# SwiGLU gate and up products as block products in seven multiplications, with the hidden layer kept in DRAM

## The chip, the cores and the metric

The kernel runs on one core of a Trainium2 chip. The metric is device time in microseconds of that core; three runs of the kernel before took 2433.13, 2434.04 and 2437.89 us, median 2434.04. A core has five engines that run side by side and meet at semaphores: TensorE (PE) multiplies, and loads its stationary operand by instructions of its own (PEld); VectorE (DVE), ScalarE (ACT) and GpSimd (POOL) do elementwise work; SyncE (SP) issues most DMAs. Each engine takes its instructions in the order in which the program has them. TensorE reads from SBUF and writes to PSUM, which has 8 banks of 512 fp32 columns.

## The reference

Two layers over 1088 tokens (1024 of a prompt, 64 of eight sample sequences), 1024 features. Layer 0 mixes by convolution and an RWKV-7 recurrence, layer 1 by causal window averages. Each is followed by a SwiGLU feed-forward network of 2816 hidden features, which is what changes here:

```
def swiglu(x, wg, wu, wd):
    return (jax.nn.silu(x @ wg) * (x @ wu)) @ wd
...
x = layer_norm(ALPHA * x + mix, p['ln_mix_g'][i], p['ln_mix_b'][i])
x = layer_norm(ALPHA * x + swiglu(x, p['ffn_gate'][i], p['ffn_up'][i], p['ffn_down'][i]),
               p['ln_ffn_g'][i], p['ln_ffn_b'][i])
```

## The kernel before

Every wide product is made of three: each operand is split into a rounded part (hi, a ScalarE copy into the type fp32r) and the rest (lo, a subtraction), and hi x hi, hi x lo and lo x hi are summed in PSUM. `split` does it for activations (subtraction on VectorE), `load_w` for weights (subtraction on GpSimd).

The program has these parts, in this order on TensorE. `phase1` and `phase2` hold the input projection, the convolution and the recurrence; phase 2 is ordered by hand on TensorE and leaves nine token tiles `y` (128 tokens by 1024 features, the last one 64 tokens) in SBUF, normalized. `feat_hl` transposes them (`ft`), applies the LayerNorm's gain and bias on ScalarE and splits them into feature-major operands for three token blocks of 384, 384 and 320 columns.

`ffn` then goes through the 22 hidden tiles in 11 groups of two. For a hidden tile and a token block, `gate_up` makes 24 products for gate (`f_g`) and 24 for up (`f_u`), silu on ScalarE, the multiplication and the split of `h` on VectorE; `down` multiplies the group's `h` by the down weights (`dn`, 512 columns wide) for all nine token tiles and adds the result to `y` on VectorE, group after group. So every weight is loaded once per layer, and `h` stays in SBUF. The first and last groups go block by block of tokens. In layer 0 the last group is followed, block by block, by `finish` (LayerNorm of the tile), `pool_tile` (layer 1's mixer: products `pp` and `pl`, with a halo of 16 tokens from the tile before) and `feat_hl` for layer 1.

The order on each engine comes from the framework's scheduler, which ranks instructions by program order and by its own estimate of when they can run; names below carry tile and group numbers. The lines of the helpers: L58 is every product, L55 every ScalarE copy, L74 the weight subtraction, L79 the activation subtraction, L1001 the product with silu, L1029 the addition to `y`, L114 gain and bias of `y` on GpSimd, L92, L98, L108 and L109 the LayerNorm.

Of the kernel before, what the change touches and what calls it, by code (L numbers as in the profile page):

```python
# [21 lines left out]
TOK = SEQ + NS * LS  # L22
FF = 2816
# [21 lines left out]
class Prog:  # L45
# [11 lines left out]
    def mm(self, out, lhsT, rhs, start=True, stop=True):  # L57
        self.nc.tensor.matmul(out, lhsT, rhs, start=start, stop=stop)  # L58
# [22 lines left out]
    def rsqrt_var(self, out, var, eps, n, name):  # L81
        """out[:, :n] = (var + eps) ** -0.5"""
# [22 lines left out]
    def layernorm(self, y, n, g, b, name):  # L105
        """y[:n] <- LayerNorm over its 1024 columns"""
# [4 lines left out]
    def affine(self, y, n, g, b, engs):  # L111
        """y[:n] <- y * gain + bias (token-major, both broadcast over the tokens)"""
# [3 lines left out]
    def load_gb(self, which):  # L116
        g = self.gb.tile([128, D], F32, tag="g", name=f"g_{which}")
        b = self.gb.tile([128, D], F32, tag="b", name=f"b_{which}")
# [4 lines left out]
    def feat_hl(self, blk, which, xb):  # L123
        """feature-major (hi, lo) of LayerNorm number `which` of the normalized y tiles of a block"""
        nc = self.nc
        n0, n = NBLK[blk]
        xh, xl = xb[blk]
        for k in range(KT):
            ps = self.psum("o" if which else "ch", f"ft{which}_{blk}_{k}")
            for i in range(3 * blk, 3 * blk + 3):  # L130
                t0, m = TT_TILES[i]
                nc.tensor.transpose(ps[:, t0 - n0:t0 - n0 + m], self.y[i][:m, k * 128:(k + 1) * 128], self.ident[:m, :m])
            t = self.ftmp.tile([128, 384], F32, tag="ft", name=f"fx{which}_{blk}_{k}")
            nc.scalar.activation(out=t[:, :n], in_=ps[:, :n], func=AF.Identity, scale=self.v("lng", which * 8 + k),
                                 bias=self.v("lnb", which * 8 + k))
            self.split(xh[:, k, :], xl[:, k, :], t[:, :n])
# [16 lines left out]
    # ------------------------------------------------------------------ consts  # L153
    def consts(self, es):
# [5 lines left out]
        self.wraw = pool("wraw", 2)  # L160
        self.wring, self.wi = [pool("wring", 2)], 0
        self.first = {4: self.load_w(I["w_in"][4].rearrange("p k f -> p (k f)"), "in4", nc.vector)}
        self.ident = cp.tile([128, 128], F32, name="ident")
# [10 lines left out]
    # ------------------------------------------------------------------ phase 1  # L174
    def phase1(self):
# [3 lines left out]
        # 0.5 * (w0, a0, ka, conv ln gain, conv ln bias, conv taps); 1 - 0.5 * ka  # L179
# [48 lines left out]
        def conv_tile(ct):  # L228
            # the tanh of the gate is written where the product with the values then goes
# [32 lines left out]
            with tc.high_priority(offset=-self.LATE):  # L262
# [6 lines left out]
                # the sample tokens: all taps of 2 sequences at once  # L269
# [100 lines left out]
    def conv_b(self, i):  # L370
        """affine part and silu, feature-major, (hi, lo)"""
# [20 lines left out]
    def wout(self, i, get, w, alpha, after=None):  # L392
        """y[i] <- alpha * y[i] + half of the output projection (alpha None: 1)"""
# [25 lines left out]
    def convs(self, wA):  # L419
        """the steps of the conv branch, in one slot per token tile and two more, each stage a slot behind the one before"""  # L420
# [560 lines left out]
    def ffn(self, l, xb, affine, finish, after):  # L981
# [49 lines left out]
        for gi, fs in enumerate(groups):  # L1031
# [11 lines left out]
            if last:  # L1043
                ldown()
                for b in range(3):
                    for f in fs:
                        gate_up(f, b, w[f, "gate"], w[f, "up"])
                    for i in range(3 * b, 3 * b + 3):
                        down(fs, i, wd, last)
                        if i == 8:  # L1050
                            self.fold(l)
# [270 lines left out]
```

## Time and profile before

| | us |
|---|---|
| median of three runs | 2434.04 |
| span of the profiled execution, first to last instruction | 2432.7 |
| TensorE busy | 2312.4 (95%) |
| VectorE busy | 1206.4 (50%) |
| GpSimd busy | 863.9 (36%) |
| ScalarE busy | 622.3 (26%) |

The profiled execution is one run of the same program; its span leaves out what lies before the first and behind the last instruction. A share of 95% for TensorE is a mean over parts that differ: in the feed-forward parts it is busy without a gap, in the recurrence it often waits. A busy time counts overlapping products once, so the price of a product is read from how often one starts, not from its own duration. The page's chain gives the path that ended last: dn 22%, f_u 21%, f_g 21%, all on TensorE.

### The profile page before, as it was taken

To read this page: it belongs to the slowest core of one execution; us is meant where nothing else is said; L and a number is where in the kernel's file an instruction comes from. 1 tells how busy PE (TensorE), PEld (TensorE's weight loads), DVE (VectorE), ACT (ScalarE), POOL (GpSimd) and SP (SyncE) were. 2 spreads that over 40 slices of the span, in tenths; PEclk is the share of its full clock that TensorE was granted. 3 is DMA by queue.
4 is the path that set the end of the run, shared out by engine and by line. 5 is a ranking of instruction groups with operands and counts; after the bars stand their busy time and mean duration, and the time that the engine had idled before them with its cause. 6 is when DMAs were issued, how large, how long until landed. Compare 5 with 4: busy or idle time off the path is not lost.

```text
span 2432.7 us, 34066 instructions
## 1 busy us (share of the span) xinstructions
PE 2312.4 (95%) x13970; PEld 2087.6 (86%) x13970; DVE 1206.4 (50%) x1907; ACT 622.3 (26%) x1273; POOL 863.9 (36%) x729
## 2 busy tenths in 40 slices
PE   8898898869988999999999999999999999999997
PEld 7887786757756999999999999898999999999996
DVE  6987798725688432223333234884232333222337
ACT  3243345445525211111111111242111111111110
POOL 3589866543317412222211222455221211222212
PEclk9998898869989999999999999999999999999999
DMA  5132427735411211111111110112111111111101
GB/s 164 47 119 70 127 77 233 229 80 154 128 48 52 76 35 53 53 35 53 40 48 35 53 52 21 53 35 70 53 48 40 53 35 35 53 53 35 52 18 74
DMA packets 132199, 169.56 MB, mean 70 GB/s; under 512 B 52229, under 2 KB 99517, under 8 KB 132036
## 3 DMA queue, kind: packets, MB, share of 16 engines
q1 hardware_dynamic: 128990, 160.15, 21.5%
q10 hardware_dynamic: 3054, 7.24, 0.8%
q8 instruction: 109, 1.79, 0.3%
q14 instruction: 46, 0.38, 0.0%
HBM read 133.43 MB, written 34.15 MB: 69 GB/s over the span
## 4 chain that ended last, share of the span: by engine, by line
PE 75%; DVE 12%; POOL 5%; issue 3%; ACT 2%; DMA 2%; SPq 0%; POOLq 0%; DVEq 0%; ACTq 0%
PE dn L58 22%; PE f_u L58 21%; PE f_g L58 21%; DVE acc L268 4%; PE wo L58 2%; PE in L58 1%; PE pp L58 1%; PE po_t L58 1%; POOL X L620 1%; PE pl L58 1%; POOL xt L618 1%; DVE f38l L79 1%; DVE xt L618 1%; DVE f40l L79 1%; PE pc_t L58 1%
## 5 line engine op out<-in xcount | busy, mean ns | idle before, releaser
L58 PE MATMUL dn<-hl_d,h 128*128 128x512 f32 (+1 forms) x2288 | 565.4, 395 | 1.6 <-DVE y L1029 1.6
L58 PEld LDWEIGHTS dn<-hl_d,h 128*128 128x128 f32 (+1 forms) x2288 | 420.3, 186 | 94.0 <-DVE y L1029 2.5
L1029 DVE TENSOR_TENSOR y<-y,dn 128x512 f32<-128x512 f32 x360 | 231.0, 682 | 323.6 <-PE dn L58 322.2
L1001 DVE TENSOR_TENSOR sg<-sg,f_u 128x384 f32<-128x384 f32 x132 | 70.1, 531 | 564.6 <-PE f_u L58 558.3
L74 POOL TENSOR_TENSOR hl_d<-raw_d,hl_d 128x1024 fp32r<-128x1024 f32 x44 | 111.6, 2558 | 529.5 <-ACT hl_d L55 529.5
L58 PE MATMUL in<-xh,hl_in 128*128 128x384 f32 (+1 forms) x1056 | 282.4, 348 | 17.4 <-ACT xh L55 9.0
L74 POOL TENSOR_TENSOR hl_gate<-raw_gate,hl_gate 128x1024 fp32r<-128x1024 f32 x44 | 106.1, 2412 | 513.4 <-ACT hl_gate L55 513.4
L1000 ACT ACTIVATE sg<-f_g 128x384 f32<-128x384 f32 x132 | 62.4, 473 | 669.1 <-PE f_g L58 669.0
L58 PEld LDWEIGHTS in<-xh,hl_in 128*128 128x128 f32 x1056 | 199.1, 201 | 30.0 <-ACT xh L55 9.0
L79 DVE TENSOR_TENSOR h<-sg,h 128x384 fp32r<-128x384 f32 (+2 forms) x176 | 166.4, 964 | 81.0 <-ACT h L55 81.0
L268 DVE SCALAR_TENSOR_TENSOR acc<-u,hv,acc 128x1024 f32<-128x1024 f32 x120 | 193.2, 1620 | 0.8
L58 PE MATMUL in<-xl,hl_in 128*128 128x384 f32 (+1 forms) x528 | 182.9, 346 | 0.5 <-DVE xl L79 0.5
L55 ACT ACTIVATE h<-sg 128x384 fp32r<-128x384 f32 (+2 forms) x176 | 70.4, 423 | 314.6 <-DVE sg L1001 314.6
L74 POOL TENSOR_TENSOR hl_up<-raw_up,hl_up 128x1024 fp32r<-128x1024 f32 x44 | 105.9, 2407 | 36.5 <-ACT hl_up L55 36.4
L58 PEld LDWEIGHTS in<-xl,hl_in 128*128 128x128 f32 x528 | 105.5, 200 | 3.6 <-issue 1.8
L58 PE MATMUL f_g<-f37h,hl_gate 128*128 128x384 f32 x352 | 95.9, 342 | 2.3 <-ACT sg L1000 1.2
L58 PE MATMUL f_u<-f37h,hl_up 128*128 128x384 f32 x352 | 97.7, 337 | 0.0
L58 PE MATMUL f_u<-f43h,hl_up 128*128 128x384 f32 x352 | 97.1, 337 | 0.0
L58 PE MATMUL f_u<-f39h,hl_up 128*128 128x384 f32 x352 | 95.8, 342 | 0.0
L58 PE MATMUL f_g<-f43h,hl_gate 128*128 128x384 f32 x352 | 94.9, 339 | 0.0
L58 PE MATMUL f_g<-f39h,hl_gate 128*128 128x384 f32 x352 | 94.6, 338 | 0.0
L58 PE MATMUL f_g<-f45h,hl_gate 128*128 128x384 f32 x352 | 94.1, 338 | 0.0
(428 smaller groups left out, 4803.9 us busy)
## 6 DMA issues: line engine op xcount, KB each, us to landing
raw_gate<-ffn_gate SPq DMA_DIRECT2D x44, 512.0 KB
raw_up<-ffn_up SPq DMA_DIRECT2D x44, 512.0 KB
raw_d<-ffn_down SPq DMA_DIRECT2D x44, 512.0 KB
raw_in<-w_in SPq DMA_DIRECT2D x22, 512.0 KB
ATm_t<-atd SPq DMA_DIRECT2D x16, 512.0 KB
y<-x SPq DMA_DIRECT2D x8, 512.0 KB
AR_t<-ard SPq DMA_DIRECT2D x8, 512.0 KB
BKh_t<-bkd SPq DMA_DIRECT2D x8, 512.0 KB
```

The lines of the kernel that those rows point to most:

```text
L55: self.nc.scalar.activation(out=out, in_=in_, func=AF.Copy)
L58: self.nc.tensor.matmul(out, lhsT, rhs, start=start, stop=stop)
L74: (eng or nc.gpsimd).tensor_tensor(out=hl[:, 1, :], in0=raw, in1=hl[:, 0, :].bitcast(F32), op=ALU.subtract)
L79: (eng or self.nc.vector).tensor_tensor(out=out_lo, in0=src, in1=out_hi.bitcast(F32), op=ALU.subtract)
L268: nc.vector.scalar_tensor_tensor(out=out, in0=src, scalar=cw(j), in1=out, op0=ALU.mult, op1=ALU.add)
L618: eng.tensor_tensor(out=xs, in0=X[:P, :m, s:s + 1].to_broadcast([P, m, w]), in1=At[:P, s:s + 1, s + 1:].to_broadcast([P, m, w]), op=ALU.mult)
L620: eng.tensor_tensor(out=nx, in0=nx, in1=xs, op=ALU.add)
L1000: nc.scalar.activation(out=t, in_=pg[0][:, :n], func=AF.Silu)
L1001: nc.vector.tensor_tensor(out=t, in0=t, in1=pg[1][:, :n], op=ALU.mult)
L1029: nc.vector.tensor_tensor(out=ys, in0=ys, in1=ps[half][:n], op=ALU.add)
```

## The change

The two weight matrices and the activations of the gate and up products are cut into 2 x 2 blocks: a pair of hidden tiles (2 x 128 features) by two halves of the 1024 input features, and two halves of the input features by two halves of the tokens (544 each). The product of the blocks is made with Strassen's scheme in Winograd's form: seven block products instead of eight, with four sums of weight blocks (`s1` to `s4`, per pair and matrix) and four of activation blocks (`t1` to `t4`, per layer). Every block product is again hi x hi, hi x lo, lo x hi, on two PSUM banks of 272 columns.

`h` is written to DRAM tile by tile (`hd`). The down products come after all of gate and up: three groups of three token tiles, each with its sums in six PSUM banks over all 22 hidden tiles, and for every group the down weights are loaded and split again. Between phases, `y` and its transposed form go through DRAM as well (`yd`, `xtd`), where before they stayed in SBUF.

```
+    def product(self, ps, op, x, start, stop):
+        for k in range(4):
+            for i, (a, b) in enumerate(((0, 0), (0, 1), (1, 0))):
+                for s in range(2):
+                    self.mm(ps[s][:, :TQ], op[:, a, k * 128:(k + 1) * 128], x[:, b, k, s * TQ:(s + 1) * TQ],
+                            start and k == 0 and i == 0, stop and k == 3 and i == 2, skip_group_check=not start)
+    def operand(self, src, name):
+        hl = self.hlp.tile([128, 2, 512], F32R, tag="op", name=f"op_{name}")
+        self.split(hl[:, 0, :], hl[:, 1, :], src)
+        return hl
+    def late_x(self, l, pool):
...
+        for k in range(4):
+            xf = [self.rawp.tile([128, 2, TH], F32, tag="rw", name=f"xl{l}_{k}{j}") for j in range(2)]
+            for j in range(2):
+                nc.sync.dma_start(out=xf[j], in_=self.xtd[l][j][:, k::4, :])
...
+            t1 = diff("t1", xf[1][:, 0], xf[0][:, 0])
+            t2 = diff("t2", xf[1][:, 1], t1)
+            diff("t3", xf[1][:, 1], xf[1][:, 0])
+            put("b22", xf[1][:, 1])
+            diff("t4", xf[0][:, 1], t2)
+    def emit(self, l, p, mat, blk, s, src):
...
+            nc.scalar.activation(out=self.sg[key], in_=src, func=AF.Silu)
+        else:
+            t = self.sg.pop(key)
+            nc.vector.tensor_tensor(out=t, in0=t, in1=src, op=ALU.mult)
+            c0 = (blk % 2) * TH + s * TQ
+            nc.scalar.dma_start(out=self.hd[l][2 * p + blk // 2][:, c0:c0 + TQ], in_=t)
+    def first_two(self, l, p, mat, a11, a12, between=None):
...
+        pa = [self.psum("mm", f"pa{nm}{s}") for s in range(2)]
+        self.product(pa, self.operand(a11, f"a11_{nm}"), self.X["b11"], True, True)
...
+            self.copy_act(c1[s], pa[s][:, :TQ])
...
+        self.product(pa, self.operand(a12, f"a12_{nm}"), self.X["b21"], False, True)
+    def gate_up(self, l, p, mat, c1=None):
...
+            s1 = comb("s1", a21, a22, ALU.add)
+            s2 = comb("s2", s1, a11, ALU.subtract)
...
+            self.product(ps["b"], self.operand(s2, f"s2_{nm}"), X["t2"], True, True)
...
+                nc.vector.tensor_tensor(out=u2[s], in0=c1[s], in1=ps["b"][s][:, :TQ], op=ALU.add)
+            self.product(ps["c"], self.operand(s1, f"s1_{nm}"), X["t1"], True, True)
...
+                self.copy_act(c5[s], ps["c"][s][:, :TQ])
...
+        self.product(ps["b"], self.operand(s3, f"s3_{nm}"), X["t3"], False, True)
...
+        self.product(ps["c"], self.operand(s4, f"s4_{nm}"), X["b22"], False, True)
+        for s in range(2):
+            out(3, s, c5[s], u3[s])
+            out(1, s, u2[s], ps["c"][s][:, :TQ])
+        self.product(pd, self.operand(a22, f"a22_{nm}"), X["t4"], True, True)
+        for s in range(2):
+            out(2, s, u3[s], pd[s][:, :TQ])
+    EARLY = 2
+    def stage1_early(self, l):
+        self.early_x(l)
+        for p in range(self.EARLY):
+            for mat in ("gate", "up"):
...
+                self.c1[p, mat] = self.first_two(l, p, mat, raw[:, :512], raw[:, 512:])
+    def stage2(self, l, gb, finish):
...
+        for g in ((0, 1, 2), (3, 4, 5), (6, 7, 8)):
...
+                ps[i] = [self.psum(("mm", "o", "ch")[j], f"dn{l}_{i}_{x}") for x in range(2)]
+                self.y[i] = self.yp.tile([128, D], F32, tag="y", name=f"yr{l}_{i}")
+                nc.sync.dma_start(out=self.y[i][:TT_TILES[i][1]], in_=self.yd[l][i][:TT_TILES[i][1]])
+                self.affine(self.y[i], TT_TILES[i][1], *gb, (nc.gpsimd, nc.gpsimd))
+            for f in range(NF):
...
+                nc.sync.dma_start(out=raw, in_=I["ffn_down"][l, f])
+                wd = self.wdp.tile([128, 2, 1024], F32R, tag="wd", name=f"hl_d{l}_{f}_{t0}")
+                self.split(wd[:, 0, :], wd[:, 1, :], raw)
...
+                nc.sync.dma_start(out=hr[:, :n], in_=self.hd[l][f][:, t0:t0 + n])
...
     def build(self):
...
+            e1.close()
+            self.rawp = pool("raws", 4)
+            self.hlp = pool("ops", 7)
...
+            for l in range(2):
+                self.stage1_early(l)
+                self.stage1(l)
...
+                    if l == 0:
+                        self.pool_weights(self.gb)
...
+                    self.stage2(l, g0, finish)
```

`early_x` loads and splits the two blocks that need only the first half of the tokens (`b11`, `b21`); `first_two` of the first two pairs uses these alone, and comes ahead of `late_x`. `finish` holds the LayerNorm of a tile and, in layer 0, `pool_tile`, the normalization and `xt` (transposes, gain and bias, the write to `xtd`).

The first place at which the order changes is TensorE where the recurrence ends and the first feed-forward part begins. Before, with `wo` the output projection of the last token tile, `ft` the transposes and `f_0_0_g` the gate products of the first hidden tile and token block:

```order
L58 MATMUL wo_36_7322<-hl_woB_5467,bhl_7323 64x512
L132 MATMUL ft_0_2_7433<-ident,y_3956 128x128
L132 MATMUL ft_0_2_7433<-ident,y_3957 128x128
L132 MATMUL ft_0_2_7433<-ident,y_3958 128x128
...
L58 MATMUL f_0_0_g<-f37h_7411,hl_gate_0_7614 128x384
L58 MATMUL f_0_0_g<-f38l_7412,hl_gate_0_7614 128x384
L58 MATMUL f_0_0_g<-f37h_7411,hl_gate_0_7614 128x384 x2
```

Now, with `xt_8` the transposes of the last token tile and `pa_0g` the first block product of gate:

```order
L60 MATMUL wo_36_7551<-hl_woB_5533,bhl_7552 64x512
L135 MATMUL xt_7_0_7594<-ident,y_4029 128x128
...
L135 MATMUL xt_8_0_7617<-ident,y_4030 128x64
L135 MATMUL xt_8_1_7628<-ident,y_4030 128x64
...
L60 MATMUL pa_0g_7697<-b_0_7669,op_a_0_0g 128x272
L60 MATMUL pa_0g_7698<-b_0_7669,op_a_0_0g 128x272
```

Before, gate products of the first block start while later tiles are still being transposed; now the first block product stands behind the transposes of the last tile.

The second place is ScalarE where layer 0's gate and up end and the down products begin. Before, around a group of down products, `hl_d` are the down weights and `h` the hidden tile:

```order
L55 ACTIVATE hl_gate_3_8152<-raw_gate_3_8150 128x1024
L55 ACTIVATE hl_up_3_8157<-raw_up_3_8155 128x1024
L1000 ACTIVATE sg_2_0_8211<-f_2_0_g 128x384
L55 ACTIVATE hl_d_2_8502<-raw_d_2_8500 128x1024
L55 ACTIVATE hl_d_3_8507<-raw_d_3_8505 128x1024
L55 ACTIVATE h_2_0_8210<-sg_2_0_8211 128x384
```

Now, at the change of stage, with `hd` the writes of `h` and `hl_pw` the mixer's weights of layer 1:

```order
L1069 DMA hd_20_116<-sg_10_11_12949 128x272
L57 ACTIVATE hl_d_0_0_13310<-raw_d_0_0_13308 128x1024
L57 ACTIVATE hl_d_1_0_13338<-raw_d_1_0_13336 128x1024
L1069 DMA hd_21_117<-sg_10_20_12981 128x272
L1069 DMA hd_21_117<-sg_10_21_12984 128x272
L57 ACTIVATE hl_pw_13281<-raw_pw_13274 128x1024
L57 ACTIVATE hl_pw_13285<-raw_pw_13276 128x1024
L57 ACTIVATE h_0_0_13315<-hr_0_0_13313 128x384
```

The copy of the first hidden tile, `h_0_0`, now stands behind the last writes of `h` and behind the mixer's weights.

The third place is TensorE behind the last down products of layer 0. Before, with `pp` and `pl` the mixer's products for the last tile and `f_1_0` the products of layer 1's first hidden tile:

```order
L58 MATMUL f_1_0_u<-f43h_12979,hl_up_1_14272 128x384
L58 MATMUL pl_0_13985<-hl_pw_12973,phl_1_14006 64x256 x2
L58 MATMUL f_1_0_u<-f43h_12979,hl_up_1_14272 128x384
L58 MATMUL f_1_0_u<-f44l_12980,hl_up_1_14272 128x384
L58 MATMUL pl_0_13985<-hl_pw_12973,phl_1_14006 64x256
L58 MATMUL pl_0_13985<-hl_pw_12976,phl_1_14006 64x256 x3
```

Now, at tile 6, with `pa_1u` the last of the early block products:

```order
L60 MATMUL pp_0_15875<-c_pm,yr_6_15228 128x144 x2
L60 MATMUL pp_0_15875<-halo_15128,ident 128x16 x2
L60 MATMUL pa_1u_16437<-b_1_16211,op_a_1_1u 128x272 x12
L60 MATMUL pa_1u_16438<-b_1_16211,op_a_1_1u 128x272 x12
L60 MATMUL pl_0_15874<-hl_pw_13281,phl_0_15881 128x256 x3
...
L135 MATMUL xt_8_0_16182<-ident,yr_8_15240 128x64
L60 MATMUL pb_0g_16605<-t_1_16504,op_s_1_0g 128x272
```

Before, products of layer 1 are mixed in until the last tile; now the early products are used up at tile 6, and tiles 6 to 8 stand alone in front of the first product that needs `late_x` (`pb_0g`).

## Rows read from the trace of the kernel before

**Rows 1.** The page's head: the span, then each engine's busy time.
```profile
span 2432.7 us, 34066 instructions
...
PE 2312.4 (95%) x13970; PEld 2087.6 (86%) x13970; DVE 1206.4 (50%) x1907; ACT 622.3 (26%) x1273; POOL 863.9 (36%) x729
```

**Rows 2.** Stretches: us, busy PE, PEld, DVE, ACT, POOL; clock, DMA share, GB/s.
```profile
340.00:460.00 120.00, 99.49 (x480) 83.44 (x481) 103.54 (x225) 61.06 (x141) 72.40 (x94) 0.79 0.61 186
960.00:1440.00 480.00, 480.00 (x2618) 446.78 (x2617) 147.88 (x215) 79.23 (x133) 97.95 (x40) 1.00 0.14 44
```

**Rows 3.** Chain of waits around 1880 us: start us, us, what, count.
```profile
1866.65 4.22 PE f_g L58 x24
...
1883.54 3.52 PE f_g L58 x24
...
1890.58 5.57 PE dn L58 x24
```

**Rows 4.** Groups by line on TensorE: count | busy us, mean ns | idle before.
```profile
L58 PE MATMUL dn<-hl_d,h 128*128 128x512 f32 (+1 forms) x2288 | 565.4, 395 | 1.6 <-DVE y L1029 1.6
```

**Rows 5.** Tiles hl_gate and pl: ns min/median/max, first and last start us.
```profile
L58 PE MATMUL f_g<-f37h,hl_gate x352: 331/336/687, 733.5 to 1489.6; 128*128 128x384 f32 x176
...
L58 PE MATMUL pl<-hl_pw,phl x216: 274/281/561, 1536.1 to 1640.2; 128*128 128x256 f32 x96, 128*64 128x256 f32 x12
```

**Rows 6.** TensorE in order of time in the mixer: start us, us, what, count.
```profile
1588.67 0.96 PE L58 MATMUL pl<-hl_pw,phl 128*128 128x256 f32 x6
...
1590.33 0.95 PE L58 MATMUL pl<-hl_pw,phl 128*128 128x256 f32 x6
1591.12 0.29 PE L58 MATMUL pp<-c_pm,y 128*128 128x144 f32 x1
```

**Rows 7.** Groups by shape on VectorE: count | busy us, mean ns | idle before.
```profile
L1029 DVE TENSOR_TENSOR y<-y,dn 128x512 f32<-128x512 f32 x360 | 231.0, 682 | 323.6 <-PE dn L58 322.2
...
L1001 DVE TENSOR_TENSOR sg<-sg,f_u 128x384 f32<-128x384 f32 x88 | 48.7, 553 | 361.4 <-PE f_u L58 356.7 <-ACT fx L134 4.7
...
L108 DVE SCALAR_TENSOR_TENSOR y<-y,mv_f,g 128x1024 f32<-128x1024 f32 x16 | 21.8, 1361 | 0.0
L1001 DVE TENSOR_TENSOR sg<-sg,f_u 128x320 f32<-128x320 f32 x44 | 21.4, 486 | 203.3 <-PE f_u L58 201.6 <-ACT sg L1000 1.7
...
L98 DVE BATCH_NORM_STATS2 st_f<-y 128x6 f32<-128x512 f32 x32 | 20.9, 682 | 0.0
...
L79 DVE TENSOR_TENSOR bhl<-bt_t,bhl 128x512 fp32r<-128x512 f32 x8 | 5.5, 687 | 0.1
...
L74 DVE TENSOR_TENSOR hl_woA<-raw_woA,hl_woA 128x1024 fp32r<-128x1024 f32 x4 | 4.9, 1215 | 0.0
```

**Rows 8.** VectorE in order of time, 770 to 784 us: start us, us, what.
```profile
772.71 2.69 DVE L79 TENSOR_TENSOR f40l<-fx,f39h 128x384 fp32r<-128x384 f32 x1
...
782.98 0.56 DVE L79 TENSOR_TENSOR h<-sg,h 128x384 fp32r<-128x384 f32 x1 [0.19 <-ACT h L55]
```

**Rows 9.** GpSimd in order of time, the same stretch: start us, us, what.
```profile
772.33 7.88 POOL L114 TENSOR_TENSOR y<-y,b 128x1024 f32<-128x1024 f32 x3
```

**Rows 10.** Groups by shape on ScalarE: count | busy us, mean ns | idle before.
```profile
L55 ACT ACTIVATE hl_d<-raw_d 128x1024 fp32r<-128x1024 f32 x44 | 44.3, 1052 | 176.4 <-PE dn L58 176.4
```

**Rows 11.** End of the recurrence, TensorE in order of time: start us, us, what.
```profile
724.43 7.33 PE L58 MATMUL wo<-hl_woB,bhl 128*64 128x512 f32 x24 [2.28 <-ACT bhl L55]
```

**Rows 12.** End of the recurrence, VectorE in order of time: start us, us, what.
```profile
735.31 0.15 DVE L86 TENSOR_SCALAR rs_m<-mv_m 64x1 f32<-64x1 f32 x1
735.38 5.03 DVE L79 TENSOR_TENSOR f38l<-fx,f37h 128x384 fp32r<-128x384 f32 x2
740.33 0.80 DVE L92 TENSOR_SCALAR y<-y,mv_m,rstd_m 64x1024 f32<-64x1024 f32 x1
```

**Rows 13.** End of the program in order of time: start us, us, what.
```profile
2418.70 1.21 PE L58 MATMUL dn<-hl_d,h 128*128 128x512 f32 x4 [1.03 <-DVE y L1029]
...
2427.28 1.28 DVE L109 SCALAR_TENSOR_TENSOR y<-y,rstd_f,b 64x1024 f32<-64x1024 f32 x1 [0.44 <-POOL rstd_f L87]
```

More of the change, by code (lines that the diff above doesn't have):

```diff
@@ L121, in load_gb, with xt @@
         return g, b
-    def feat_hl(self, blk, which, xb):
+    def xt(self, l, i, y, pool):
         nc = self.nc
[L126 to L136, printed above, removed]
+        t0, n = TT_TILES[i]
+        nc.scalar.dma_start(out=self.yd[l][i][:n], in_=y[:n])
+        for q in range(2):
+            xo = pool.tile([128, 4, 128], F32, tag="t", name=f"xo{l}_{i}_{q}")
+            ps = self.psum("tp", f"xt{l}_{i}_{q}")
+            for k in range(4):
+                nc.tensor.transpose(ps[:, k * 128:k * 128 + n], y[:n, (4 * q + k) * 128:(4 * q + k + 1) * 128], self.ident[:n, :n])
+                nc.scalar.activation(out=xo[:, k, :n], in_=ps[:, k * 128:k * 128 + n], func=AF.Identity,
+                                     scale=self.v("lng", 16 * l + 4 * q + k), bias=self.v("lnb", 16 * l + 4 * q + k))
+            for j in range(2):
+                a, b = max(t0, j * TH), min(t0 + n, (j + 1) * TH)
+                if a < b:
+                    nc.scalar.dma_start(out=self.xtd[l][j][:, 4 * q:4 * q + 4, a - j * TH:b - j * TH], in_=xo[:, :, a - t0:b - t0])
     _u = 0
@@ new lines, in load_pair, with half @@
+    def load_pair(self, l, p, mat):
+        raws = []
+        for f in (2 * p, 2 * p + 1):
+            raw = self.rawp.tile([128, 2, TH], F32, tag="rw", name=f"raw_{mat}{l}_{f}").rearrange("p a b -> p (a b)")[:, :1024]
+            self.nc.sync.dma_start(out=raw, in_=self.I["ffn_" + mat][l, f].rearrange("p k f -> p (k f)"))
+            raws.append(raw)
+        return [raws[0][:, :512], raws[0][:, 512:], raws[1][:, :512], raws[1][:, 512:]]
+    def half(self, tag, name, bufs=None):
+        kw = {} if bufs is None else {"bufs": bufs}
+        return self.tmp1.tile([128, TQ], F32, tag=tag, name=name, **kw)
@@ new lines, in emit @@
+    def emit(self, l, p, mat, blk, s, src):
+        nc = self.nc
+        key = p, blk, s
+        if mat == "gate":
+            if key not in self.sg:
+                self.sg[key] = self.half("sg", f"sg{l}_{p}_{blk}{s}", 10)
+            nc.scalar.activation(out=self.sg[key], in_=src, func=AF.Silu)
[4 more added lines that the diff above has]
+            nc.scalar.dma_start(out=self.hd[l][2 * p + blk // 2][:, c0:c0 + TQ], in_=t)
@@ L1064, in fold @@
     def fold(self, l):
         nc, y = self.nc, self.y[8]
-        ps = [self.psum("o", f"fold{l}_{x}") for x in range(2)]
+        ps = [self.psum("tp", f"fold{l}_{x}") for x in range(2)]
         for half in range(2):
@@ L1152, in pool_tile @@
                             c == 0 and a == 0 and w == 0, c == 1 and a == 1)
[L1153 to L1156 removed]
+            if gi % 2:
+                ys = y[:n, (gi // 2) * 512:(gi // 2 + 1) * 512]
+                nc.vector.scalar_tensor_tensor(out=ys, in0=ys, scalar=ALPHA, in1=po[:n], op0=ALU.mult, op1=ALU.add)
     def build(self):
@@ L1184, in build @@
-            self.foldm = self.phl.tile([128, 64], F32, tag="fold", name="foldm", bufs=1)
-            nc.sync.dma_start(out=self.foldm, in_=I["fold"])
-            nc.gpsimd.memset(self.y[8][64:, :], 0.0)
-            gb = self.load_gb(0)
-            xb = blocks()
-            for blk in range(3):
-                self.feat_hl(blk, 0, xb)
-            gf = []
-            xb2 = []
-            def fin0(i):
-                if not gf:
-                    gf.append(self.load_gb(1))
-                self.layernorm(self.y[i], TT_TILES[i][1], *gf[0], f"f0_{i}")
```

298 lines of the change are left out of this document (163 added, 135 removed).

## The prediction, made before the changed kernel ran

> **What bounds the kernel now.** First the page's head: TensorE is busy 95% of the span, every other engine at most half of it [rows 1]. A share is a mean, so next come the stretches. In the 480 us from 960 to 1440 TensorE is never idle at the full clock, while VectorE is busy for 148 us, GpSimd for 98 and ScalarE for 79 [rows 2]. The chain of waits there is nothing but 24 products of gate or up at a time, and 24 of down [rows 3]: TensorE alone sets the pace, and a product costs what its columns cost. 24 products of 384 columns take 4.22 us, 24 of 320 take 3.52, 24 of 512 take 5.57: 0.458, 0.458 and 0.453 ns a column. A hidden tile and matrix takes 4.22 + 4.22 + 3.52 = 11.96 us, and there are 22 x 2 x 2 = 88: 1052.5 us. The 2288 down products [rows 4] take 0.2321 each, 531.0 us. The first gate product starts at 733.5 [rows 5], the last down product ends at 2418.70 + 1.21 = 2419.9 [rows 13]: of these 1686.4 us the products fill 1583.5, and 102.9 are left for layer 1's mixer, transposes and idle time.
>
> **Gate and up.** Per pair of hidden tiles and matrix, 7 block products of 4 x 3 x 2 = 24 products of 272 columns replace 2 x 72 wider ones: 44 x 168 = 7392. No row has 272 columns. At 0.4583 ns a column one takes 124.7 ns, in all 921.5: 131.0 us less. From above: 147 ns, as the 320-column ones, would make 1084 (163 more than I take). Six of 256 columns take 1591.12 - 1590.33 = 0.79 us [rows 6], 132 ns each, which scaled to 272 is 140: 1035, or 113 more. From below nothing excludes a gain, but rows from 320 to 512 columns lie within 1% of one rate. I take 124.7, since two widths agree exactly and the six stand behind a switch from the mixer's plain fp32 products, which the block products don't have.
>
> What lies beside them: per pair (41.9 us of TensorE) VectorE has 14 operand splits and 8 weight sums of 512 columns at 0.687, and 28 operations of 272 columns out of PSUM. These I price at 0.436, from 486 at 320 and 553 at 384 [rows 7]. Sum 27.3 us, 65%. ScalarE has 14 copies of half of 1052 ns [rows 10], 16 of about 0.4 and 8 DMA issues, some 17 us. GpSimd has nothing to do there. In the order the operands of a block product are made four to seven products (12 to 20 us) ahead, so I cost all this at nothing; if that cover fails by 1 us per pair and matrix, it costs 44 us.
>
> **Down.** The 2288 products stay. The weights are loaded and split three times: 132 steps per kernel instead of 44 loads. A step is 18 products, 4.18 us (16 in the last group). Beside it VectorE needs 1.215 for the weights [rows 7] and 0.56 for h [rows 8], ScalarE 1.05 [rows 10] and about 0.5, and the DMAs bring 524 + 197 KB: 172 GB/s. The trace moves 44 GB/s at a share of 0.14, so 314 at full load, and has run at 186 [rows 2]. Hidden, with 2.4 us to spare on VectorE. The 396 additions to y at 682 ns become 36; they were off the path and give nothing back.
>
> **Where the parts meet.** The mean gain is only as good as these places, none of which the trace shows; I take them in order of time.
>
> Start. Now the first block product stands behind the last transposes, and its operands' memory is freed only when phase 2 is done with y. The recurrence's last output projection ends at 724.43 + 7.33 = 731.8 [rows 11], and the last tile's statistics are ready at 735.46; its normalization then waits for two subtractions of 5.03 us [rows 12] that go, so y is ready near 737, not 741. From the end of the last VectorE instruction (2428.56) to the end of the span are 4.1 us, with one DMA in them [rows 13]; I price every trip to or from DRAM by that. Write y 4.1, load x 4.1, split 1.2, load the weights into the freed buffers 4.1, split 2.5: first product at 753, against 733.5. The early products fill 4 x 48 x 0.1247 = 24 us. Meanwhile VectorE has 8 splits and 36 operations of late_x of 544 columns (0.687 + 32 columns, 0.72), 8 splits of 512 and 4 others: 39 us from 745 on, so all operands stand at 786. TensorE has 24 us done and about 7 of what the first quarters allow (bounds 0 and 33), and the remaining 461 - 31 = 430 run dense: 1216.
>
> Change of stage. The last 1.7 us of VectorE's work on h come first, then in its order two weight splits and the split of h_0_0. In that time GpSimd has 12 operations for the mixer's weights and four y tiles in layer 0 (8 in layer 1). Beside such an operation of 2.6 us [rows 9] a subtraction of 384 columns takes 2.69, without it 0.56 [rows 8]. So 1.7 + 3 x 2.7 = 9.8 us, and for the rest of GpSimd's 31 us each step needs 5.4 instead of 4.18, some 4 more: 14 in layer 0, 10 in layer 1. The copy of h_0_0 also waits on ScalarE behind the mixer's weights, which wait for GpSimd; the DMA writes behind it are not needed for the first products. Bounds: 4.7 (no contention) to 31 (until GpSimd is done). The Trainium skill, "SBUF — State Buffer", section Who interferes with whom, says that a VectorE instruction with two SBUF inputs and a GpSimd one that reads SBUF exclude each other for a whole instruction; the trace agrees (2.69 against 0.56). By the rule a 1024-column split would wait 2.6 and then take 1.2, and the change of stage would cost 16 and 12.
>
> Down stage, layer 0: 1144 x 0.2321 = 265.5. In its order the mixer and transposes of tiles 0 to 3 lie between the down products: one of a tile's four rounds takes 1590.33 - 1588.67 = 1.66 us [rows 6], 6.6 a tile, and about 1 for the transposes: 30. At each of two group changes VectorE has 6 evictions at 682, 6 statistics at 682 and 6 LayerNorm halves at 1361 among its splits [rows 7], 16 us more in four steps that leave it 2.4 each: 6 lost. Tile 5 gets its y buffer only after tile 1's transposes: load 4.1, GpSimd 5.2, eviction 1.4, against 5 of work: 6 lost. Sum 265.5 + 30 + 18, end at 1216 + 14 + 313.5 = 1543.5.
>
> Next layer. In the order tiles 4 to 8 are still to be mixed. Nine tiles took 1640.2 - 1536.1 = 104 us before [rows 5], 11.6 each: 58. Then write and load 8.2, late_x 26: operands at 1636, with 31 us of TensorE's work done as above. Stage 1 ends at 2066, the change of stage costs 10, the down stage 265.5 + 12: 2353.5.
>
> End. Before, 12.8 us lie behind the last down product. Now three tiles finish together: 3 x 5.8 of VectorE, 2.8 earlier for the first, the fold 2, the DMA 4.1: 21. Span 2374.5. The median stands 1.3 above the profile's span, so I forecast 2375.
>
> **Rivals.**
> *The meeting places cost little.* VectorE is half idle, the scheduler may have packed it well; without the 24 of the changes of stage, the 30 in the down stages, and 10 of the mixer: 2311. Against it: contention is in the rows.
> *VectorE falls behind.* For it: in-order waits on PSUM between operand splits. 44 us as worked out: 2419.
> *Down stage bound by supply, slower than before.* Place: each of the 132 steps; price: 0.72 MB of DMA and two splits that must come round within two buffers. The forecast leaves 59 us, so it decides from a step of 4.18 + 59/132 = 4.63 us, 156 GB/s. At 128 GB/s a step takes 5.6, 188 more: 2563. Against it: 186 GB/s at a share of 0.61 [rows 2].
> *272 columns are no cheaper than 320.* Then seven products save nothing, the change does not do what it says: 2375 + 163 = 2538. Against it: the proportional rows.
>
> **How the numbers follow.** Forecast 0.55, with its own range 2340 to 2405; little cost 0.18; VectorE behind 0.14; supply 0.08; no cheaper columns 0.05. Both slower cases lie above 2440; leaving them out leaves 13 in 100, and with the lower case cut at 2305 the range 2305 to 2440 holds 8 in 10. About 0.2%, 5 us, is what a measurement here tells from no change. Faster is the sum of the first three less a tail: 0.85; slower 0.11; same 0.04.
>
> **What would show it.** Right: block products starting every 125 ns in runs of 168; in stage 1 TensorE without gaps and VectorE near 65%; a step of the down stage 4.2 us; gaps of TensorE of some 20 to 40 us at three places, the largest in front of `pb_0g` of layer 1, with VectorE on late_x; subtractions of 2.7 us at both changes of stage. Wrong: products at 140 ns or more; VectorE or a DMA as the releaser of block products in the middle of stage 1; steps over 4.6 us; or a mixer of tiles 4 to 8 that takes over 80 us.

## The result: slower by 5%, and the profile after

The changed kernel takes 2552.44 us (median of four runs, 2549.05 to 2555.08), the kernel before 2433.59 in the same comparison: a ratio of 1.049, 95% interval 1.047 to 1.052. The forecast was 2375 us, with a range of 2305 to 2440. The profiled execution has a span of 2551.2.

The page's head, the profile after (span; busy time, share and instructions of each engine; two lines of the groups by line), answers to [rows 1] and [rows 4]:

```profile
span 2551.2 us, 39001 instructions
...
PE 2255.3 (88%) x15026; PEld 2007.6 (79%) x15026; DVE 1558.7 (61%) x2687; ACT 903.7 (35%) x1909; POOL 545.1 (21%) x591
...
L60 PE MATMUL dn<-hl_d,h 128*128 128x512 f32 (+1 forms) x2288 | 545.3, 397 | 49.1 <-ACT h L57 37.4
...
L116 POOL TENSOR_TENSOR yr<-yr,g 128x1024 f32<-128x1024 f32 (+1 forms) x18 | 47.8, 2665 | 595.3 <-DMA yr<-yd 574.2
```

TensorE is busy for 57 us less than before, as a change that saves multiplications should make it, and yet the span is 118 us longer: it now waits for some 296 us instead of 120. Three stretches of the changed kernel say where (us, then busy time of PE, PEld, DVE, ACT, POOL; granted clock, DMA share, GB/s), and answer to [rows 2]:

```profile
860.00:1240.00 380.00, 380.00 (x3035) 380.00 (x3035) 230.87 (x464) 123.00 (x268) 0.00 (x0) 1.00 0.25 79
1700.00:1760.00 60.00, 41.07 (x139) 29.46 (x139) 14.87 (x28) 12.30 (x32) 2.61 (x3) 0.50 0.16 48
1760.00:1793.00 33.00, 0.51 (x2) 0.20 (x2) 24.72 (x39) 13.60 (x24) 0.00 (x0) 0.50 0.58 190
```

In the first, the block products, nothing waits: 380 / 3035 = 125.2 ns a product (forecast 124.7), VectorE busy 61% (forecast 65). In the second TensorE mixes the last tiles of layer 1 alone, at half the clock. In the third it stands still for 33 us, until VectorE has prepared x for the block products.

The program's milestones, from the first and last instruction of each kind on TensorE, against the terms of the prediction:

| stretch | forecast, us | measured, us | off by |
|---|---|---|---|
| start to first block product of layer 0 | 753 | 801.4 | +48 |
| to the last block product | 463 | 477.4 | +14 |
| change of stage, layer 0 | 14 | 18.4 | +4 |
| down stage with mixer tiles 0 to 3 | 313.5 | 314.4 | +1 |
| rest of the mixer, and operands for all block products | 92.5 | 181.7 | +89 |
| what is left of the block products of layer 1 | 430 | 440.9 | +11 |
| change of stage, layer 1 | 10 | 14.3 | +4 |
| down stage, layer 1 | 277.5 | 283.3 | +6 |
| end | 21 | 19.3 | -2 |

The span is 177 us over the forecast's 2374.5. Two rows hold 138 of them: the start, and the passage from layer 0 to layer 1.

**The start.** The recurrence itself ends later: its last output projection ends at 786.1 instead of 731.8 [rows 11], and the waits from 600 to 690 us name the transposes `xt` (engine, line, releaser: us in total, times, longest):

```profile
PEld xt L135 <- ACT xo L136: 24.4, 24, 1.9
...
PE xt L135 <- ACT xo L136: 18.0, 24, 1.5
```

The same stretch in order of time, PE and ACT:

```profile
621.75 0.47 PE L135 MATMUL xt<-ident,y 128*128 128x128 f32 x1 [1.52 <-ACT xo L136]
622.26 0.46 ACT L136 ACTIVATE xo<-xt,vec 128x128 f32<-128x128 f32 x1 [0.57 <-PE xt L135]
...
622.77 0.48 PE L135 MATMUL xt<-ident,y 128*128 128x128 f32 x1 [0.55 <-ACT xo L136]
623.29 0.46 ACT L136 ACTIVATE xo<-xt,vec 128x128 f32<-128x128 f32 x1 [0.57 <-PE xt L135]
```

Line 133 takes one PSUM tile for four transposes, and line 136 copies each out right behind it. A transpose waits until the copy of its neighbour is through, and the copy waits for the transpose: 1.02 us a pair, some 8 us of TensorE for a token tile. Seven of the nine tiles stand in TensorE's in-order queue in front of parts of the recurrence. The Trainium skill, "PSUM — Partial Sum Buffer", section PSUM bank collisions raise a hardware error, says that two engines must not touch one bank in the same partitions at once, disjoint columns or not; the trace agrees, in the rows above no transpose runs beside a copy out of its tile.

**From layer 0 to layer 1.** The mixer of one tile near its end, TensorE in order of time (start us, us, what; in brackets the idle time before and what ended it):

```profile
1706.44 1.68 PE L60 MATMUL pl<-hl_pw,phl 128*128 128x256 f32 x6 [0.47 <-ACT phl L57]
1707.92 1.05 PE L60 MATMUL pp<-c_pm,yr 128*128 128x128 f32 x4
1708.76 0.87 PE L60 MATMUL pp<-halo,ident 128*128 128x16 f32 x4
1710.11 1.68 PE L60 MATMUL pl<-hl_pw,phl 128*128 128x256 f32 x6 [0.47 <-ACT phl L57]
...
1717.46 1.68 PE L60 MATMUL pl<-hl_pw,phl 128*128 128x256 f32 x6 [0.47 <-ACT phl L57]
1722.65 0.66 PE L135 MATMUL xt<-ident,yr 128*128 128x128 f32 x2 [3.51 <-DVE yr L94]
```

A round takes 3.67 us, at a granted clock of 0.50; the prediction took 1.66 from [rows 6], at the full clock. Behind four rounds TensorE waits 3.51 for the tile's normalization, then come its transposes, and only then the next tile. The kernel before, in its mixer:

```profile
1586.84 0.42 PE L132 MATMUL ft<-ident,y 128*128 128x128 f32 x2
1587.02 0.96 PE L58 MATMUL pl<-hl_pw,phl 128*128 128x256 f32 x6
...
1600.29 0.51 PE L58 MATMUL f_g<-f43h,hl_gate 128*128 128x384 f32 x2
1600.64 0.39 PE L58 MATMUL pl<-hl_pw,phl 128*128 128x256 f32 x2
...
1601.22 0.33 PE L58 MATMUL f_u<-f44l,hl_up 128*128 128x384 f32 x1
...
1601.57 0.64 PE L58 MATMUL pl<-hl_pw,phl 128*128 128x256 f32 x4
1602.04 0.41 PE L58 MATMUL pp<-c_pm,y 128*128 128x144 f32 x2
```

There the transposes (`ft`) stand a few at a time between the rounds, and the rounds hardly wait: from 1574.0 to 1592.0 the `pl` products of two tiles pass, in 10.3 and 7.7 us, with no gate, up or down product beside them; TensorE is busy for 16.3 of the 18 us, at the full clock but for 3.4. Gate and up products of layer 1 (`f_g`, `f_u`) run among the last tiles' mixing, from 1594.2 on: the first token block needs the first three tiles alone. A block product of the seven needs differences of the first and second half of all tokens, so that beyond the first two products of a pair nothing can start before the last tile is mixed. The change put a barrier between the layers. Behind it, the chain of waits (start us, us, what):

```profile
1761.18 2.10 DMA xtd<-xo
...
1763.33 4.09 DMA xl<-xtd
...
1788.76 0.72 DVE t4f L1036
...
1791.99 0.61 DVE s_0g L1096
...
1793.31 1.28 PE pb_0g L60 x4
```

A trip through DRAM, 36 operations of `late_x` on VectorE, the first sums: 33 us in which TensorE has nothing, its early products having been spent between 1657 and 1690. The forecast had 34 us for this part of the row; all of the 89 us lie in the mixing before it.

### The profile page after: what moved, and what is told of

The parts are those of the page before. It is cut to its first block, busy times and chain, and to the rows that moved or that the text cites. A ratio compares the mean times of both kernels' runs of the same rounds, so it can differ in the third digit from the quotient of the medians.

```text
span 2551.2 us, 39001 instructions
## 1 busy us (share of the span) xinstructions
PE 2255.3 (88%) x15026; PEld 2007.6 (79%) x15026; DVE 1558.7 (61%) x2687; ACT 903.7 (35%) x1909; POOL 545.1 (21%) x591
## 5 line engine op out<-in xcount | busy, mean ns | idle before, releaser
L81 DVE TENSOR_TENSOR hl_d<-raw_d,hl_d 128x1024 fp32r<-128x1024 f32 x132 | 178.6, 1354 | 205.2 <-ACT hl_d L57 205.0
L57 ACT ACTIVATE hl_d<-raw_d 128x1024 fp32r<-128x1024 f32 x132 | 139.8, 1060 | 345.5 <-PE dn L60 313.5
L116 POOL TENSOR_TENSOR yr<-yr,g 128x1024 f32<-128x1024 f32 (+1 forms) x18 | 47.8, 2665 | 595.3 <-DMA yr<-yd 574.2
L81 DVE TENSOR_TENSOR h<-hr,h 128x384 fp32r<-128x384 f32 (+2 forms) x176 | 107.4, 631 | 34.7 <-ACT h L57 34.5
L136 ACT ACTIVATE xo<-xt,vec 128x128 f32<-128x128 f32 (+1 forms) x144 | 59.7, 447 | 74.1 <-PE xt L135 73.1
L57 ACT ACTIVATE h<-hr 128x384 fp32r<-128x384 f32 (+2 forms) x176 | 68.9, 415 | 28.0 <-DMA hr<-hd 27.6
L60 PE MATMUL wo<-hl_woB,bhl 128*128 128x512 f32 (+1 forms) x216 | 70.0, 473 | 2.3 <-ACT bhl L57 2.2
L60 PE MATMUL pl<-hl_pw,phl 128*128 128x256 f32 (+1 forms) x216 | 48.4, 361 | 21.9 <-ACT phl L57 13.2
L76 POOL TENSOR_TENSOR hl_in<-raw_in,hl_in 128x1024 fp32r<-128x1024 f32 x21 | 57.8, 2754 | 15.8 <-ACT hl_in L57 15.8
L60 PEld LDWEIGHTS wo<-hl_woB,bhl 128*128 128x128 f32 (+1 forms) x216 | 44.7, 219 | 16.5 <-ACT bhl L57 3.0
```

The lines of the kernel that those rows point to most:

```text
L57: self.nc.scalar.activation(out=out, in_=in_, func=AF.Copy)
L76: (eng or nc.gpsimd).tensor_tensor(out=hl[:, 1, :], in0=raw, in1=hl[:, 0, :].bitcast(F32), op=ALU.subtract)
L81: (eng or self.nc.vector).tensor_tensor(out=out_lo, in0=src, in1=out_hi.bitcast(F32), op=ALU.subtract)
L116: eng.tensor_tensor(out=y[:n], in0=y[:n], in1=t[:n], op=op)
L136: nc.scalar.activation(out=xo[:, k, :n], in_=ps[:, k * 128:k * 128 + n], func=AF.Identity, scale=self.v("lng", 16 * l + 4 * q + k), bias=s ...
```

## Experiments

Eleven kernels ran. Each starts from the changed kernel or from the one named. b_early0, c_setup_late, d_defer and i_setup_dve ran once each; the four runs of the changed kernel lie 6 us apart, so less than that tells nothing in their totals.

### a_xt_batch: the transposes first, then the copies

```
                 nc.tensor.transpose(ps[:, k * 128:k * 128 + n], ...)
+            for k in range(4):
                 nc.scalar.activation(out=xo[:, k, :n], in_=ps[:, k * 128:k * 128 + n], ...)
```

> The four transposes of half a token tile are issued together, and the four copies out of PSUM behind them; nothing else changes. Theory (lockstep): in the changed kernel each transpose of xt waits for ScalarE's copy of the one before, 1.03 us a round instead of 0.33 to 0.48, about 8 us of TensorE a token tile; nine tiles of it stand in TensorE's queue in front of the recurrence and push its last output projection from 731.8 to 786.1. Without it that projection ends at 735 to 745, the first block product starts near 755 instead of 801, and the mixer of layer 1 loses another 10 to 20: 2480 to 2495 in all. Rival (the work itself): what delays the recurrence is 72 copies, the DMA issues and the waits for y wherever they stand, so the projection still ends after 775 and the time is above 2530.

Measured: 2486.07 us, 66 less; against the kernel before 1.023, interval 1.021 to 1.025. The last output projection ends at 744.5, the first block product starts at 757.7. Layer 0's down stage and what follows up to the last block product of layer 1 take 27 less. ScalarE and TensorE in order of time:

```profile
615.11 0.66 PE L135 MATMUL xt<-ident,y 128*128 128x128 f32 x4 [0.74 <-ACT xo L137]
616.89 1.85 ACT L137 ACTIVATE xo<-xt,vec 128x128 f32<-128x128 f32 x5
```

Four transposes in 0.66 us, for one wait. The 72 copies, the DMAs and the place in the queue are unchanged: the rival falls, and the 48 us of the first row are settled but for some 5.

### b_early0: no early products

```
-    EARLY = 2
+    EARLY = 0
```

> EARLY is 0 in place of 2: no products are made ahead of late_x. Theory: the early products of layer 1 stand in TensorE's in-order queue between the mixer's rounds and push the last tiles back by what they take (24 us), and those of layer 0 start only when all transposes are through, so they give little: 2540 to 2565. Rival: each layer's early products fill 24 us in which TensorE would be idle: 2590 to 2600.

Measured: 2572.59 us, 20 more, between the two theories. From the end of the transposes to the last block product layer 0 takes 494.0 instead of 479.2, so there the 24 us of early products gave 15. From the last down product to the last block product of layer 1 it is 629.7 instead of 622.6: there they gave 7, as the mixer ended 13 us sooner without them.

### c_setup_late: the loads of a group behind its fourth step

```
             for f in range(NF):
+                if f == 4:
+                    if g[0] == 0:
+                        setup()          # gains, mixer constants and weights
+                    for i in g:
+                        ...              # load y, gain and bias on GpSimd
```

> The loads of y, gains, mixer constants and weights of a group are issued behind its fourth step instead of ahead of its first. Theory: the 18.3 us between the last block product and the first down product of layer 0 (14.3 in layer 1) are the SP queue, where 12 loads stand ahead of the first load of h, and ScalarE's queue, where a mixer weight's copy stands ahead of h's; they fall to 8 to 10 in both layers: 2536 to 2544. Rival (contention of VectorE and GpSimd, as predicted): the subtractions of h stay near 2.7 us and the gap shrinks by less than 3 us: 2547 to 2555.

Measured: 2549.13 us, within the runs of the changed kernel. The gap at the change of stage fell from 18.4 to 3.0 us in layer 0 and from 14.3 to 3.1 in layer 1, further than either theory had it:

```profile
1283.83 1.17 PE L60 MATMUL pd_10u<-t,op_a_10u 128*128 128x272 f32 x8
1288.04 2.47 PE L60 MATMUL dn<-hl_d,h 128*128 128x512 f32 x5 [3.04 <-ACT h L57]
```

So the gap was the queues. The trace of the changed kernel says the same: VectorE stands idle for 14.7 us there, waiting for the copy of h on ScalarE, so the gap holds hardly any contention. In that kernel 13 other loads stand on SP ahead of the first of h, with waits for earlier DMAs among them (DMA issues of SP in order of time):

```profile
1278.87 0.33 SPq L121 DMA_DIRECT2D g<-lnv  x1
...
1286.15 0.36 SPq L1239 DMA_DIRECT2D pscale<-pool_scale  x1
...
1289.36 0.91 SPq L1180 DMA_DIRECT2D hr<-hd  x2
```

and on ScalarE its copy stands behind those of the mixer's weights:

```profile
1295.64 1.06 ACT L57 ACTIVATE hl_pw<-raw_pw 128x1024 fp32r<-128x1024 f32 x1 [1.24 <-POOL raw_pw L1242]
1296.60 0.92 ACT L57 ACTIVATE h<-hr 128x384 fp32r<-128x384 f32 x2
```

But the down stages grew by 11.4 and 6.3, and VectorE of c_setup_late in order of time says why:

```profile
1326.98 3.40 DVE L81 TENSOR_TENSOR hl_d<-raw_d,hl_d 128x1024 fp32r<-128x1024 f32 x1
1330.31 2.73 DVE L81 TENSOR_TENSOR h<-hr,h 128x384 fp32r<-128x384 f32 x1
```

A step needs 6.1 us of VectorE beside GpSimd, and TensorE needs 4.2. What the queues gave, contention took back.

### i_setup_dve: that work on VectorE

The gain and bias on y, one tile each at steps 4, 8 and 12, and the mixer weights:

```
-            self.affine(self.y[i], TT_TILES[i][1], *self.g0, (nc.gpsimd, nc.gpsimd))
+            self.affine(self.y[i], TT_TILES[i][1], *self.g0, (nc.vector, nc.vector))
-    nc.gpsimd.tensor_tensor(out=raws[c], in0=raws[c], in1=sc, op=ALU.mult)
+    nc.vector.tensor_tensor(out=raws[c], in0=raws[c], in1=sc, op=ALU.mult)
```

> As c_setup_late, but the gain and bias on y and the scaling and splitting of the mixer weights run on VectorE instead of GpSimd, one tile at steps 4, 8 and 12. Theory (contention paid later): in c_setup_late the gap at the change of stage fell from 18 to 3 us, but the down stage of layer 0 grew from 314 to 326 and that of layer 1 from 283 to 290, since its splits ran beside GpSimd's operations (3.4 and 2.7 us in place of 1.2 and 0.56). Without GpSimd there they stay at 1.2 and 0.56, and the down stages fall back to 305 to 312 and 276 to 280: 2525 to 2538. Rival (loads late): the stages grew because the loads come late; VectorE now has 2 x 1.3 us more a tile and they stay where they are: 2545 to 2555.

Measured: 2525.97 us. The same two operations on VectorE, with GpSimd idle:

```profile
1314.95 1.21 DVE L81 TENSOR_TENSOR hl_d<-raw_d,hl_d 128x1024 fp32r<-128x1024 f32 x1
1316.09 0.55 DVE L81 TENSOR_TENSOR h<-hr,h 128x384 fp32r<-128x384 f32 x1
```

1.76 us for both instead of 6.13. Layer 1's down stage fell to 271.1, better than hoped. Layer 0's is 321.3, which the theory had at 305 to 312: there the mixer's weights and the gains all fall on VectorE within 20 us of its first steps. The edit also spreads the tiles over three steps, which was not tried apart. But in layer 1's down stage the subtractions of c_setup_late exceed 1.21 and 0.55 us by 32 us in sum, those of this kernel by 0.8, and TensorE idles for 16.6 us there against 6.2. So contention is shown as the cause in layer 1, where 18.5 us came back; in layer 0 only 4.5 came back.

### d_defer: the transposes of a tile behind the mixing of the next

```
                             self.pool_tile(i)
+                            if i:
+                                self.xt(1, i - 1, self.y[i - 1], self.xop)
                             self.normalize(self.y[i], n, f"m1_{i}")
-                            self.xt(1, i, self.y[i], self.xop)
```

> In layer 1's mixer the transposes of a token tile are issued behind the mixing of the next tile. Theory (turns of TensorE): each of the last five tiles costs about 30 us because TensorE, in order, waits for the tile's normalization (4 us) and the transposes in lockstep (4 us) before it may mix the next; deferred, the last five tiles take 25 to 35 us less: 2517 to 2528. Rival (chain inside a tile): products at half the clock, copies, subtractions and contention with GpSimd within each round set the pace, and it changes by less than 10: 2542 to 2555.

Measured: 2531.22 us, although its recurrence happened to end 8 us later (794.3; in the kernels that leave it alone that end lay between 786.1 and 794.3). From the last down product of layer 0 to the last transpose it is 105.1 us instead of 148.9, while the down stage took 15 more: 29 net, as the theory of turns has it.

### e_combo: a, i and d in one

> a_xt_batch, i_setup_dve and d_defer in one. Theory: the three causes lie in different places, so the gains add: 2486 for the transposes, 15 to 30 less at and behind the two changes of stage, 15 to 20 less in the mixer of the last five tiles (less than the 29 of d_defer, since the lockstep is gone already): 2436 to 2456. Rival: the gains overlap, since what the mixer gains in the down stage it loses at its tail, where TensorE runs at half the clock: 2460 to 2480.

Measured: 2436.94 us (10 runs), ratio 1.0013, interval 0.9997 to 1.0029: no change against the kernel before. The gains add (66, 26 and 21 us one by one); the three causes make up 115 of the 119 us by which the change was slower.

### f_early_after: the early products of layer 1 behind the last transposes

```
+                if l:
+                    with tc.issue_after(self.last_xt.ins):
+                        self.stage1_early(l)
```

> e_combo, with the early products of layer 1 queued on TensorE behind the transposes of the last token tile instead of between the mixer's rounds. Theory: there they hide under late_x (30 us on VectorE with TensorE idle) instead of pushing the mixer back; without them in front the mixer's tail was 13 us shorter in b_early0: 10 to 20 less than e_combo. Rival: the mixer's tail hid them for nothing, at any place they take the same: within 5 of e_combo, or slower.

Measured: 2432.37 us, ratio 0.9997, interval 0.9980 to 1.0013. Between the last down product of layer 0 and the last block product it gained 4 us (565.6 against 569.6), so the rival is right: where the early products stand matters little once the rest is mended. Why they had cost the mixer 13 us in the changed kernel (b_early0) and cost it 5 here (90.6 against 85.3) was not tried apart.

### h_all: sums of the first pair ahead of late_x

```
+            self.ahead[0, "gate"] = self.gate_up(l, 0, "gate", "ahead")
             self.late_x(l, pool)
```

> f_early_after, with the sums s1 and s2 of the first gate pair and their operands made ahead of late_x on VectorE, so that the first product behind late_x need not wait for them. Theory: 3 to 6 us in each layer, 6 to 12 less than f_early_after, which would put it below the kernel before (2432): 2405 to 2430. Rival: they are made later or earlier, VectorE is the pace there, and the sum of its work is the same: within 4 of f_early_after.

Measured: 2440.63 us, 8 more than f_early_after, ratio 1.0038, interval 1.0022 to 1.0055. Neither theory. Stage 1 of layer 0 took 485.2 instead of 479.7, and in layer 1 the way from the last down product of layer 0 to the last block product 568.7 instead of 565.6; the edit also lets both sums' operands be made before the first subtraction out of PSUM in every pair. What of that costs the time was not tried.

### l_warm and m_warm_start: TensorE kept at work

Products of the identity with itself into a free PSUM tile, which nothing reads (l_warm); and such products in front of the first block product (m_warm_start):

```
+    def warm(self, n, tag, behind=None):
+        with self.tc.issue_after((behind or self.last_mm).ins):
+            ps = self.psum(tag, f"warm{self.uid()}")
+            for _ in range(n):
+                self.nc.tensor.matmul(ps[:, :128], self.ident, self.ident, start=True, stop=True)
```

> f_early_after, with TensorE kept at work where it waits in the mixer of the last three token tiles: products of the identity with itself into a free PSUM tile, which nobody reads, 45 behind the last down product of layer 0, 24 behind the fold and 4 in each of the 12 rounds. Theory (clock): those three tiles take 85 us because TensorE, waiting there, is granted half the clock (0.54 in 1576 to 1660), so a round takes 3.67 us where the kernel before took 1.66 at the full clock; kept busy it is granted more, the rounds take 2 to 2.8 us, and the stretch 55 to 65: 2398 to 2414. Rival (chain): copy, subtraction and products of a round wait for each other at any clock, and 117 more instructions in the queue cost what they take: 2432 to 2450.

> l_warm, and 36 such products behind the last transpose of layer 0, in front of the first block product. Theory (clock): the clock there was 0.5 to 0.66 from 755 to 770 and the early products ran at half speed; kept busy, the first products of layer 0 take less, 2 to 8 less than l_warm. Rival: VectorE's 36 operations of late_x end when they end, and the early products only wait for them: within 3 of l_warm.

Measured: 2421.92 us, ratio 0.9957, interval 0.9941 to 0.9973; with m_warm_start 2419.84, 0.9941, interval 0.9923 to 0.9959. Stretches, as above: first f_early_after, then l_warm.

```profile
1600.00:1661.00 61.00, 47.24 (x181) 37.77 (x179) 21.36 (x40) 14.76 (x41) 3.13 (x4) 0.53 0.20 60
```

```profile
1600.00:1643.00 43.00, 37.62 (x275) 32.54 (x276) 17.75 (x34) 13.01 (x37) 3.13 (x4) 0.98 0.23 70
```

The granted clock rises from 0.53 to 0.98, that is, from mostly 1.2 GHz to nearly always 2.4. A round of f_early_after takes 3.67 us (TensorE in order of time):

```profile
1614.24 1.68 PE L60 MATMUL pl<-hl_pw,phl 128*128 128x256 f32 x6 [0.47 <-ACT phl L57]
...
1617.91 1.68 PE L60 MATMUL pl<-hl_pw,phl 128*128 128x256 f32 x6 [0.47 <-ACT phl L57]
```

One of l_warm takes 2.5 to 2.7 us, although four more products stand in it (two records each):

```profile
1607.00 0.61 PE L60 MATMUL pp<-c_pm,yr 128*128 128x128 f32 x4
1607.45 0.52 PE L60 MATMUL pp<-halo,ident 128*128 128x16 f32 x4
1607.82 1.14 PE L66 MATMUL warm<-ident 128*128 128x128 f32 x8
1608.71 0.95 PE L60 MATMUL pl<-hl_pw,phl 128*128 128x256 f32 x6
```

The clock is the cause of the slow rounds. The gain is 10 us and not the 18 to 34 expected: the first tile of the three still ran at half the clock from 1584 to 1600 (0.50); the chain ahead of it goes through a load of y, the LayerNorm of three tiles, the splits of `early_x`, and a load of 4.7 us for the early products' weights, for which a copy ahead of the mixer's waits on ScalarE. The 36 products at the start gave 2 us, within what two medians can differ.

### n_best: two such products a round, the state's stores on SP

> m_warm_start, with 2 of the unread products in a round instead of 4, and the 9 stores of the mixer's state issued on SP instead of ScalarE, where they stand ahead of a round's copy. Theory: in l_warm's chain the unread products take 0.99 us of a 2.6 us round, more than the 0.5 that TensorE had waited, and the stores 3.5 us before tile 8: 6 to 12 less than m_warm_start, 2407 to 2414, if two products still hold the full clock. Rival: two products do not hold the clock, the rounds go back to 3.3 us or more, and it is slower than m_warm_start by 3 to 10.

Measured: 2418.33 us, ratio 0.9945, interval 0.9928 to 0.9963, which is m_warm_start's time. The granted clock is 0.99 from 1600 to 1637 here too, and a round takes 2.5 to 2.7 us as before: the rival falls, and so does the theory's gain. It has the lowest median, 134 us below the change as it was made and 0.55% below the kernel before.

## Why the prediction was wrong

- **Block products at 124.7 ns: right.** 125.2 measured in the stretch above, 125.8 over the 3504 products that run without a gap in each layer. At that price 7392 take 930 us, 123 less than gate and up took before (1052.5): the saving came, and was lost elsewhere. The rival of dear columns and that of VectorE falling behind are out.
- **Down stage at 4.18 us a step: right** where nothing else runs: 180 products, ten steps, take 40.8 to 44.8 us in layer 1. Supply did not bind. That layer 0's whole stage came out at 314.4 against 313.5 is in part luck: it holds the wait of each transpose for its copy, which the sum had not (8 us, since a_xt_batch takes 306.1), and products of 0.227 us (180 in 40.8) where the sum took 0.2321 (6 us less over 1144).
- **"first product at 753": wrong by 48.** The failed step is the last output projection of the recurrence, taken from [rows 11] as ending at 731.8. The prediction took the end of the recurrence as given and put the transposes at nothing there. Seven tiles of them had moved into the recurrence's queue, each with eight waits for ScalarE. a_xt_batch gives 44 of the 48 back, and 42 of the 54 by which that projection ended late.
- **"Nine tiles took 1640.2 - 1536.1 = 104 us before [rows 5], 11.6 each: 58": wrong by 89 with what follows. This is the step that failed most.** From the last down product to the last transpose it was 149 us. The price was divided out of rows whose order the change does not keep. It holds other products, but they are not what made the tiles cheap: without any beside them two tiles took 10.3 and 7.7 us. In the changed kernel a tile takes 23 to 35 us, with at most the early products beside it (the transposes of the last five begin at 1634.6, 1669.9, 1700.0, 1722.7 and 1757.2). Each tile's transposes, and the normalization that they wait for, now stand in front of the next tile's rounds. So TensorE waits, for 45 of the 149 us, and is granted half the clock from 1694.6 on, where a round takes 3.67 us instead of 1.66. Of the 149, lockstep makes 21 (a_xt_batch), the place of the transposes 44 (d_defer, which pays 15 of it back in the down stage; the waits for the normalization alone are 14), and half the clock at least the 11 that l_warm took off, net of its own products. These overlap and need not add. Gate and up products, which from 1594.2 on gave the kernel before work among its last tiles, are a cover that the change removes, as the order ahead of the prediction shows (`f_1_0_u` between the `pl` rows). What that cover was worth was tried only with the early products: 7 us (b_early0).
- **"about 7 of what the first quarters allow": nothing ran on quarters**, which is the lower bound that the prediction gave. The first block product that needs `late_x` waits for all of it. So 3504 products came behind it in each layer, in 441 us instead of 430: 7 for the quarters, 4 for products of 125.8 ns. Layer 0's other 4 lie in front of them: 36.7 us from the first early product instead of 33.
- **Changes of stage, 14 and 10: near in size by luck, wrong in mechanism.** The gaps, 18.4 and 14.3, were queues on SP and ScalarE (c_setup_late); the prediction named ScalarE's, and priced contention. Contention came behind them. By the rule of the Trainium skill ("SBUF — State Buffer", Who interferes with whom) a VectorE instruction with two SBUF inputs waits until a GpSimd one that reads SBUF is through; the trace agrees, 3.40 against 1.21 and 2.73 against 0.55. It costs at each step beside GpSimd, not in the gap alone.
- **The chances.** The rivals that would have made the kernel slower were supply, at 0.08, and dear columns, at 0.05. Neither the barrier between layers nor work that is put into the recurrence's queue was on the list, though both stood in the order of instructions. One sign of being wrong was on it and came: a mixer of tiles 4 to 8 over 80 us.
- **What stays open.** The profiled run of n_best still has a span 38 us over the forecast's: 19 at the passage between the layers (111.9 against 92.5), 24 in the two stretches of block products, 13 in layer 0's down stage and 7 at the start, less 18 at the changes of stage and 7 in layer 1's down stage and at the end. What of the 19 the barrier alone costs was not tried.

## What to carry to other kernels

A saving in one stage is bounded by what the stage before and after can still overlap with: ask of every new operand how much of the earlier work must be complete before it exists, and price the stretch that then runs alone at the clock that TensorE is granted when it waits (0.50 to 0.53 here). Take a duration per tile only from rows whose order the new kernel keeps. Transposes into parts of one PSUM tile go together, copies behind them; one transpose, one copy is a wait per transpose, in whatever queue they stand.

## What the runs showed of the hardware

- Work that nobody reads made the kernel faster: 117 to 153 products of 128 columns took 10 to 14 us off, since TensorE went from 0.53 to 0.98 of its clock where it had been waiting for copies.
- With GpSimd at work, a 1024-column subtraction on VectorE took 3.40 us instead of 1.21. Giving VectorE what GpSimd did there, so more work, one tile at a time, shortened the down stage of layer 1 from 289.6 to 271.1.
